# Reordering the seven products of a Strassen-form MLP: first product kept in PSUM, sums taken off GpSimd, norms placed under products

## The chip, the cores and the metric

One core of a Trainium2 chip runs the whole program. The metric is the device time of one execution in microseconds; the median of three runs of the kernel before is 2013.3 us (2011.71 to 2015.76). The profile is one more execution, of 2016.24 us.

## The reference

Two transformer blocks over 1024 tokens of width 1024, in float32. What the change touches is the MLP of the first block and the two norms behind it:

```python
    h = rmsnorm(x, ln2[l])
    gate, up = jnp.split(jnp.einsum('btd,df->btf', h, w_gu[l]), 2, axis=-1)   # 1024 -> 2 x 2816
    x = x + jnp.einsum('btf,fd->btd', jax.nn.silu(gate) * up, w_down[l])      # 2816 -> 1024
  return rmsnorm(x, ln_f)
  # second block begins:
  h = rmsnorm_2(x, norm_g[i]);  u = h @ w_in   # MLA projections
```

Before the MLP stand an input projection, a pooling mixer, a gated linear attention and a forgetting attention; behind it the second block's attention and its output. They are the same in both kernels.

## The kernel before, in words

A float32 product is made of three matmuls on pairs (hi, lo): every operand is cut by `split` (L181) into hi, a ScalarE cast to fp32r (L185), and lo, a VectorE subtraction (L186); hi·hi, hi·lo and lo·hi are added in PSUM.

Both halves of the MLP multiply 2x2 block matrices with seven products in place of eight (Winograd's form of Strassen). **Gate/up** (L1049 to L1360): the activations, transposed to features by tokens, are cut in two along features and along tokens; the four quarters and their sums are called A11, A12, A22, S1 to S4. `sums` (L1143) and `more_sums` (L1161) make them for four 128-token blocks, the second with GpSimd (L1164 to L1166). The weights come in 22 blocks: `gates` and `ups` load a block's raw weights, `w_sums` (L1234) makes four sums on VectorE, `cut_w` and `cut_t4` split them into a ring of four slots (two in pool `wg`, two in `mr`; a block takes three, w0 to w2, besides t4). `ahead(n + 1, step)` puts these steps for the next block between the products of the present one. `products(n)` (L1283) makes the seven products of block n, 12 matmuls of 128x128 by 128x512 each, into three PSUM banks a, b, c, in the order A11 (a), S2 (b), A12 (a), S3 (b), S1 (c), A22 (b), S4 (c). Bank a is read after A11 by a ScalarE copy, X; U2 = X + b after S2, U3 = X + b after S3, g2 = X + b after A22, and two sums with c, are VectorE additions; two SiLUs are ScalarE's. In the first two blocks S2 comes behind A12. GpSimd multiplies gate by up, makes the seven activation sums of the down half in a tile q, and SyncE's queue writes them to DRAM (`a_s`).

**Down** (L1362): seven products again, each of 11 k-blocks of 128, 12 matmuls a k-block, taken in pairs (groups g = 0 to 5, the last with one). `operands(j, g)` loads a pair of `a_s`, and splits it and the pair of weight rows; it is issued one group ahead. The raw quarters of `w_down` (B11, B21, B12, B22, 3 transfers each) and x1, the residual, come by SyncE's queue: B11 and B21 first, x1 during product 0, B22 and B12 before product 1. `sums23` and `sums41` make weight sums in place on VectorE. The first product, bank a, is copied by ScalarE and added by GpSimd to three places of x1 (L1413, twelve additions); the others are added by VectorE (L1405). Banks: a for products 0 and 1, b for 2, 3 and 6, c for 4 and 5.

**The norms.** For each 128-token block tb, `norm_f` squares on ScalarE (L202), takes the root by a tiny VectorE step and GpSimd (L203, L204), scales on VectorE (L1433) and stores x3 from ScalarE's queue; `norm_g` squares again, multiplies by a gain on GpSimd (L1439) and scales on ScalarE (L1440); `turn` makes eight TensorE transposes (L214) and four splits. tb 0 to 3 stand under product 6, tb 4 to 7 behind it. The first MLA products (token half 0 of two z blocks, 48 matmuls) need tb 0 to 3, the next (token half 1) need tb 4 to 7.

The order on each engine is set when the program is built, by a scheduler that walks the text: text order is priority, `urgent` gives more, and an instruction that is ready in the scheduler's own timing may be put ahead of one that waits. Once built, each engine's queue is fixed.

Of the kernel before, what the change touches and what calls it, by code (L numbers as in the profile page):

```python
# [25 lines left out]
def f(ap):  # L26
    return ap.bitcast(F32)
# [137 lines left out]
class K:  # L165
# [883 lines left out]
    def proj_o(self):  # L1049
# [85 lines left out]
        def cut(name, i, x):  # L1135
            o = slice(i * P, i * P + P)
            self.split(*[a[:, :, o] for a in self.hq[name]], x)
# [5 lines left out]
        def sums(i):  # L1143
# [8 lines left out]
            s3 = tp.tile([P, 4, P], F32, tag="U3", name="s3")  # L1152
            s2[i] = tp.tile([P, 4, P], F32, tag=("U2", "g2", "up", "up")[i], name="s2", bufs=(1, 1, 2, 2)[i])
# [5 lines left out]
            cut("S3", i, s3)  # L1159

        def more_sums(i):  # L1161

            a, b = both("A12", i)
# [3 lines left out]
            cut("S1", i, t[i][:, 0])  # L1167
            cut("A22", i, t[i][:, 1])
            cut("S4", i, s2[i])
        run0, run1 = self.products(0), self.products(1)  # L1170
# [6 lines left out]
        next(run0)  # L1177
# [3 lines left out]
        next(run0)  # L1181
        sums(2)
        next(run1)
        sums(3)
        next(run1)
        self.cut_t4(0)
        self.cut_w(0, 2)
        for i in range(4):
            more_sums(i)
        hp_cm.close()  # L1190
        self.tq = self.b2_cm.enter_context(self.pool("mq"))
        self.ups(1)
        self.w_sums(1)
        for j in range(2):
            self.cut_w(1, j, 1)
        for n, run in ((0, run0), (1, run1)):
            for step in range(5):
                next(run)
                if n == 0 and step == 2:
                    self.cut_w(1, 2)  # L1200
                    self.cut_t4(1)
                    self.gates(2)
                    self.ups(2)
                elif n == 1:
                    self.ahead(2, step)
            next(run, None)
# [76 lines left out]
    def products(self, n):  # L1283
# [3 lines left out]
        early = n < 2  # L1287

        def tmp(tag, bufs=1):
            return tp.tile([P, 512], F32, tag=tag, name=tag, bufs=bufs)  # L1290
        a, st = self.pm.tile([P, 512], F32, tag="mm", name="mma"), {}
        self.quarter(a, w[n][0], 0, "A11", last=False)
        X = tmp("X", 2)
        with self.urgent():
            nc.scalar.copy(X, a)
        if early:
            yield
        else:
            yield from self.inner(n, X, st, tmp, 0)
        self.quarter(a, w[n][1], 0, "A12", first=False)  # L1300
        sg = tmp("sg", 2)
        nc.scalar.activation(sg, a, AF.Silu)
        yield
        if early:
            yield from self.inner(n, X, st, tmp, 0)
        yield from self.inner(n, X, st, tmp, 1)
        b = st["b"]
        c = self.pm.tile([P, 512], F32, tag="mm", name="mmc")
        self.quarter(c, w[n][2], 0, "S1", last=False)
        up2, up1, g2 = tmp("up", 2), tmp("up", 2), tmp("g2")  # L1310
        with self.urgent():
            V.tensor_tensor(up2, st["U3"], c, ALU.add)
        yield
        self.quarter(b, w[n][3], 0, "A22", first=False)
        with self.urgent():
            V.tensor_tensor(g2, X, b, ALU.add)
        nc.scalar.activation(g2, g2, AF.Silu)
        yield
        self.quarter(c, w[n][2], 512, "S4", first=False)
        with self.urgent():  # L1320
            V.tensor_tensor(up1, st["U2"], c, ALU.add)
# [19 lines left out]
    def inner(self, n, X, st, tmp, step):  # L1341
        V, w = self.nc.vector, self.gw
        if step == 0:
# [3 lines left out]
            with self.urgent():  # L1347
                V.tensor_tensor(st["U2"], X, b, ALU.add)
# [803 lines left out]
```

## Time and profile before

| what | us |
|---|---|
| median of three runs | 2013.3 |
| the profiled execution, its time | 2016.24 |
| its span, first to last instruction | 2014.5 |
| PE busy in it | 1899.3 (94%) |
| DVE / ACT / POOL busy | 1172.8 / 853.9 / 350.6 |
| mean granted clock | 0.971 of 2.4 GHz |

The gate/up half runs from about 553 to 1013 us, the down half to about 1256 us, and the norms of the last four token blocks to about 1292 us. PE is TensorE, DVE VectorE, ACT ScalarE, POOL GpSimd, SPq SyncE's DMA queue.

### The profile page before, as it was taken

To read this page: it belongs to the slowest core of one execution; us is meant where nothing else is said; L and a number is where in the kernel's file an instruction comes from. 1 tells how busy PE (TensorE), PEld (TensorE's weight loads), DVE (VectorE), ACT (ScalarE), POOL (GpSimd) and SP (SyncE) were. 2 spreads that over 40 slices of the span, in tenths; PEclk is the share of its full clock that TensorE was granted. 3 is DMA by queue.
4 is the path that set the end of the run, shared out by engine and by line. 5 is a ranking of instruction groups with operands and counts; after the bars stand their busy time and mean duration, and the time that the engine had idled before them with its cause. 6 is when DMAs were issued, how large, how long until landed. Compare 5 with 4: busy or idle time off the path is not lost.

```text
span 2014.5 us, 26529 instructions
## 1 busy us (share of the span) xinstructions
PE 1899.3 (94%) x10046; PEld 1614.0 (80%) x10046; DVE 1172.8 (58%) x1838; ACT 853.9 (42%) x1670; POOL 350.6 (17%) x268
## 2 busy tenths in 40 slices
PE   6999899999959999999987999799999999999998
PEld 6887689987847888888875877697989999878886
DVE  6345545894387556555458556434278778783434
ACT  5412235782152232232222335522277777772322
POOL 1022210000043233242341003211101101000000
PEclk9999999999969999999998999799999999999999
DMA  5113345645113232322493233304043433527112
GB/s 180 41 42 126 105 139 129 154 102 188 42 52 110 95 120 89 105 105 99 140 345 114 96 95 107 115 23 147 14 106 93 93 75 88 129 79 246 63 43 104
DMA packets 90207, 218.48 MB, mean 108 GB/s; under 512 B 11184, under 2 KB 15200, under 8 KB 90064
## 3 DMA queue, kind: packets, MB, share of 16 engines
q1 hardware_dynamic: 84064, 203.20, 32.8%
q10 hardware_dynamic: 6016, 13.59, 2.0%
q8 instruction: 79, 1.29, 0.3%
q14 instruction: 48, 0.39, 0.1%
HBM read 145.36 MB, written 54.74 MB: 99 GB/s over the span
## 4 chain that ended last, share of the span: by engine, by line
PE 73%; DVE 8%; ACT 6%; issue 5%; DMA 4%; POOL 3%; SPq 0%; ACTq 0%; POOLq 0%; DVEq 0%
PE mm L193 11%; PE mm L195 11%; PE mm L194 11%; PE mmb L1280 9%; PE mmd L1504 7%; PE mmc L1280 5%; PE mma L1280 5%; PE O L731 4%; PE tps L706 3%; PE S L1768 1%; DVE wlo L186 1%; PE S L1769 1%; PE S L1770 1%; ACT P L697 1%; ACT pth L719 1%
## 5 line engine op out<-in xcount | busy, mean ns | idle before, releaser
L185 ACT CAST whi<-wst 128x1024 fp32r<-128x1024 f32 (+3 forms) x165 | 160.5, 978 | 370.7 <-PE mmd L1504 120.4
L186 DVE TENSOR_TENSOR wlo<-wst,whi 128x1024 fp32r<-128x1024 f32 (+3 forms) x165 | 213.1, 1295 | 174.5 <-ACT whi L185 171.3
L717 DVE TENSOR_TENSOR ptl<-tps,pth 128x512 fp32r<-128x512 f32 (+2 forms) x312 | 151.6, 519 | 24.3 <-ACT pth L719 22.4
L697 ACT ACTIVATE P<-S,m 128x128 f32<-128x128 f32 (+3 forms) x192 | 144.1, 752 | 30.1 <-DVE m L691 24.4
L691 DVE TENSOR_REDUCE m<-S 128x1 f32<-128x128 f32 (+3 forms) x192 | 140.2, 749 | 21.8 <-PE S L1770 17.0
L204 POOL TENSOR_TENSOR rr<-ss,mhalf 128x1 f32<-128x1 f32 x64 | 36.4, 572 | 663.6 <-DVE ss L203 658.9
L193 PE MATMUL mm<-t,whi 128*128 128x512 f32 x352 | 144.1, 410 | 3.7 <-ACT whi L185 3.7
L194 PE MATMUL mm<-t,whi 128*128 128x512 f32 x352 | 142.6, 405 | 0.0
L195 PE MATMUL mm<-t,wlo 128*128 128x512 f32 x352 | 142.1, 404 | 0.4 <-DVE wlo L186 0.4
L719 ACT CAST pth<-tps 128x512 fp32r<-128x512 f32 (+2 forms) x312 | 128.0, 461 | 30.3 <-PE tps L706 27.8
L1504 PE MATMUL mmd<-wlo,whi 128*128 128x512 f32 x308 | 123.4, 401 | 14.6 <-DVE wlo L186 13.8
L193 PE MATMUL mm<-whi,t 128*128 128x512 f32 (+1 forms) x336 | 126.4, 376 | 1.3 <-DVE og L999 1.0
L706 PE MATMUL tps<-ident,P 128*128 128x128 f32 x864 | 123.4, 277 | 4.1 <-DVE ptl L717 2.9
L1280 PE MATMUL mmb<-t,whi 128*128 128x512 f32 x352 | 112.8, 401 | 14.4 <-ACT t L185 12.0
L195 PE MATMUL mm<-whi,t 128*128 128x512 f32 (+1 forms) x336 | 125.0, 373 | 0.0
L1504 PE MATMUL mmd<-whi 128*128 128x512 f32 x308 | 118.6, 394 | 6.4 <-ACT whi L185 6.4
L194 PE MATMUL mm<-wlo,t 128*128 128x512 f32 (+1 forms) x336 | 124.3, 370 | 0.0
L1504 PE MATMUL mmd<-whi,wlo 128*128 128x512 f32 x308 | 122.3, 397 | 0.0
L1280 PE MATMUL mma<-t,whi 128*128 128x512 f32 x352 | 111.4, 398 | 7.9 <-DVE t L1241 7.7
L706 PEld LDWEIGHTS tps<-ident,P 128*128 128x128 f32 x864 | 97.5, 142 | 11.5 <-DVE ptl L717 2.9
L1280 PEld LDWEIGHTS mmb<-t,whi 128*128 128x128 f32 x352 | 67.4, 192 | 31.7 <-ACT t L185 12.4
L193 PEld LDWEIGHTS mm<-t,whi 128*128 128x128 f32 x352 | 68.8, 196 | 21.5 <-ACT whi L185 4.8
(395 smaller groups left out, 4821.8 us busy)
## 6 DMA issues: line engine op xcount, KB each, us to landing
as<-q SPq DMA_DIRECT2D x77, 256.0 KB
wst<-as SPq DMA_DIRECT2D x35, 512.0 KB
wst<-in_w_gu_dram SPq DMA_DIRECT2D x44, 256.0 KB
wst<-in_w_gu_dram SPq DMA_DIRECT2D x22, 512.0 KB
x<-in_x_dram SPq DMA_DIRECT2D x16, 512.0 KB
wst<-in_win_s_dram SPq DMA_DIRECT2D x14, 512.0 KB
Q<-qk SPq DMA_DIRECT2D x24, 256.0 KB
K<-qk SPq DMA_DIRECT2D x24, 256.0 KB
```

The source lines that it names most:

```text
L185: nc.scalar.copy(hi, src)
L186: nc.vector.tensor_tensor(lo, src, f(hi), ALU.subtract)
L193: mm(ps, lh, rh, start=first, stop=False)
L194: mm(ps, lh, rl, start=False, stop=False)
L195: mm(ps, ll, rh, start=False, stop=last)
L691: nc.vector.tensor_reduce(m, S[:, o:o + (i + 1) * P], axis=AX.X, op=ALU.max, negate=True)
L697: nc.scalar.activation(st["P", h, u][:, x:x + n], st["S", h, u][:, o:o + n], AF.Exp, bias=st.pop(("m", h, i)), accum_out=H[h][4][:, i:i + 1])
L706: nc.tensor.transpose(ps[:, x, :], st["P", h, u][:, o:o + P], self.ident)
L717: nc.vector.tensor_tensor(v[1], ps[:, x0:x1, :], f(v[0]), ALU.subtract)
L719: nc.scalar.copy(v[0], ps[:, x0:x1, :])
L1280: self.nc.tensor.matmul(ps, x[:, c], y[:, k, :], start=first and k + n == 0, stop=last and k == 3 and n == 2, skip_group_check=True)
L1504: nc.tensor.matmul(ps[t], x[:, ts], y[:, cs], start=start and k + i + m == 0, stop=k + i == 10 and m == 2, skip_group_check=True)
```

## The change

- **Gate/up, order.** A11 goes to bank b and stays there: X is a ScalarE copy of it, and S2, S3 and A22 are accumulated on top. A12 goes to bank a alone, and X += a is a VectorE addition before the SiLU. U2 and U3 become ScalarE copies of b, g2's SiLU reads b itself. A block reads PSUM five times by ScalarE (with SiLUs) and three by VectorE, where it was three by each with one more SiLU from SBUF and two more VectorE additions. The order is A11, A12, S2, S3, S1, A22, S4.
- **First two blocks.** Their products alternate; S1 and S4's activation sums are made by VectorE, and all that follows the sums of the fourth token block is put behind its last cut on ScalarE's and VectorE's queues.
- **Down.** Order and banks: 0 (b), 1 (a), 5 (c), 2 (b), 4 (d), 3 (b), 6 (b). The first product stays in b, product 4 is added to two places, GpSimd's twelve additions are gone. The transfers of weights and x1 are spread over the groups. k loops outside the token blocks; the last group of product 6 goes token block by token block.
- **Norms.** tb 0 to 3 stand under products 5 and 6, half a step apart; `norm_g` is one VectorE operation (no GpSimd, no ScalarE scaling); x3 is stored from SyncE's queue; three h buffers of their own.

```diff
@@ proj_o: first blocks @@
         def more_sums(i):
-            a, b = both("A12", i)
-            G.tensor_tensor(t[i][:, 0], t[i][:, 0], t[i][:, 1], ALU.add)
-            G.tensor_tensor(s2[i], a, s2[i], ALU.subtract)
-            G.tensor_tensor(s2[i], s2[i], b, ALU.add)
+            V.tensor_tensor(t[i][:, 0], t[i][:, 0], t[i][:, 1], ALU.add)
             cut("S1", i, t[i][:, 0])
-            cut("A22", i, t[i][:, 1])
+        def last_sums(i):
+            a, b = both("A12", i)
+            V.tensor_tensor(s2[i], a, s2[i], ALU.subtract)
+            V.tensor_tensor(s2[i], s2[i], b, ALU.add)
             cut("S4", i, s2[i])
...
+        act, dve = sums(3)
+        next(runs[1])
+        with self.tc.issue_after(act), self.tc.issue_after(dve):
+            self.ups(1)
+            self.w_sums(1)
+            for j in range(2):
+                self.cut_w(1, j, 1)
+            for n in range(2):
+                next(runs[n])
+                self.cut_w(n, 2)
+            for i in range(4):
+                more_sums(i)
+            for n in range(2):
+                next(runs[n])
+            self.cut_t4(0)
+            for i in range(4):
+                cut("A22", i, t[i][:, 1])
...
@@ products @@
+        self.quarter(b, w[n][0], 0, "A11", last=False)
+        X = read("X", b)
...
+            self.quarter(a, w[n][1], 0, "A12")
             yield
+        plus(X, a)
+        A.activation(X, X, AF.Silu)
         yield
+        self.quarter(b, w[n][0], 512, "S2", first=False, last=False)
+        U2 = read("U2", b)
+        yield
+        self.quarter(b, w[n][1], 512, "S3", first=False, last=False)
+        U3 = read("U3", b)
+        yield
+        c = bank("mmc")
         self.quarter(c, w[n][2], 0, "S1", last=False)
+        plus(U3, c)
         yield
         self.quarter(b, w[n][3], 0, "A22", first=False)
+            A.activation(g2, b, AF.Silu)
         yield
         self.quarter(c, w[n][2], 512, "S4", first=False)
+        plus(U2, c)
...
@@ down @@
-        plan = [(0, "B11", "a", True, first), (1, "B21", "a", False, adds(0, L)), (2, "B11", "b", True, adds(0, H)),
-                (3, "B12", "b", False, adds(4, H)), (4, "B11", "c", True, adds(4, H)),
-                (5, "B22", "c", False, adds(0, H)), (6, "B21", "b", False, adds(4, L))]
+        plan = [(0, "B11", "b", True, adds((0, L))), (1, "B21", "a", True, adds((0, L))),
+                (5, "B22", "c", True, adds((0, H))), (2, "B11", "b", False, adds((0, H))),
+                (4, "B11", "d", True, adds((0, H), (4, H))), (3, "B12", "b", False, adds((4, H))),
+                (6, "B21", "b", False, None)]
+        transfers = {(0, 0): ("B21", 0), (0, 1): ("B21", 4), (0, 2): ("B21", 8), (0, 3): (0, 1), (0, 4): (2, 3),
+                     (1, 0): ("B22", 0), (1, 1): ("B12", 0), (1, 2): ("B22", 4), (1, 3): ("B12", 4),
+                     (1, 4): ("B22", 8), (1, 5): ("B12", 8), (2, 1): (4, 5), (2, 2): (6, 7)}
...
-            nc.scalar.dma_start(self.x3_s[tb], x)
+            nc.sync.dma_start(self.x3_s[tb], x)
...
-            G.tensor_tensor(hs[tb], x1[tb], self.gn, ALU.mult)
-            nc.scalar.activation(hs[tb], hs[tb], AF.Copy, scale=r)
+            V.scalar_tensor_tensor(hs[tb], x1[tb], r, self.gn, ALU.mult, ALU.mult)
...
+                if j >= 5:
+                    norms(g + 6 * (j - 5))
...
+        for t in range(4):
+            with self.urgent():
+                V.tensor_tensor(x1[4 + t][:, L], x1[4 + t][:, L], ps[t], ALU.add)
```

## Rows read from the trace of the kernel before

**Rows 1.** The head of the profile page: the span, TensorE's busy time, and TensorE's granted clock in 40 equal slices of the span (tenths of full speed).

```profile
span 2014.5 us, 26529 instructions
PE 1899.3 (94%) x10046; PEld 1614.0 (80%) x10046; DVE 1172.8 (58%) x1838; ACT 853.9 (42%) x1670; POOL 350.6 (17%) x268
...
PEclk9999999999969999999998999799999999999999
```

**Rows 2.** The view of busy time by stretches, six stretches of the two MLP halves. Columns: the stretch (us from the span's start), its length, then busy us (and instructions) of PE, weight loads, DVE, ACT, POOL, then the granted clock, the share of the DMA engines, GB/s.

```profile
553.40:626.10 72.70, 49.70 (x194) 37.81 (x193) 58.76 (x72) 31.59 (x51) 28.52 (x17) 0.79 0.21 69
626.10:1010.00 383.90, 382.87 (x1668) 312.52 (x1667) 218.28 (x252) 109.53 (x137) 127.95 (x80) 1.00 0.31 110
1013.40:1043.60 30.20, 30.20 (x133) 24.59 (x131) 11.05 (x10) 9.95 (x12) 7.88 (x7) 1.00 0.85 324
1043.60:1071.70 28.10, 9.83 (x30) 6.93 (x29) 26.26 (x15) 6.47 (x7) 22.41 (x12) 0.70 0.66 242
1096.00:1245.00 149.00, 147.10 (x648) 119.47 (x646) 89.15 (x94) 61.90 (x72) 8.93 (x7) 1.00 0.30 97
1256.30:1292.20 35.90, 21.00 (x89) 16.37 (x89) 17.41 (x26) 21.43 (x34) 15.00 (x13) 0.74 0.37 124
```

**Rows 3.** The view of waits of PE over the whole span: who waited for whom, us in total, times, the longest.

```profile
PE mmd L1504 <- DVE wlo L186: 13.8, 5, 10.1
PE mmb L1280 <- ACT t L185: 12.0, 1, 12.0
PE tps L214 <- ACT h L1440: 11.0, 4, 5.6
```

**Rows 4.** Timeline rows of the first two blocks of gate/up, six moments: start us, length us, engine, line, operation; in brackets the idle time before it and what ended it.

```profile
556.92 0.68 DVE L1155 TENSOR_TENSOR s<-t,ht 128x512 f32<-128x512 f32 x1
...
562.48 1.75 DVE L1239 TENSOR_TENSOR wst<-wst 128x512 f32<-128x512 f32 x1
...
567.49 0.68 DVE L1242 TENSOR_TENSOR wst<-wst 128x512 f32<-128x512 f32 x1
...
581.52 0.69 DVE L186 TENSOR_TENSOR t<-s,t 128x512 fp32r<-128x512 f32 x1 [4.92 <-ACT t L185]
...
579.13 0.62 ACT L185 CAST vh<-s 128x512 fp32r<-128x512 f32 x1 [2.93 <-POOL s L1166]
...
590.33 0.79 PE L1280 MATMUL mmb<-t,whi 128*128 128x512 f32 x1 [11.98 <-ACT t L185]
```

**Rows 5.** Timeline of PE around the read of U2 in the second block: the last of four S1 products, and the first S3 products after it.

```profile
613.96 0.39 PE L1280 MATMUL mmc<-uh,whi 128*128 128x512 f32 x1
616.12 0.73 PE L1280 MATMUL mmb<-t,whi 128*128 128x512 f32 x2 [1.77 <-DVE U L1348]
```

**Rows 6.** The view of the tile mma: its copy by ScalarE (min/median/max ns); then the timeline row of PE that followed such a copy directly.

```profile
L1295 ACT COPY X<-mma x22: 586/587/591, 556.6 to 997.1; 128x512 f32<-128x512 f32 x22
...
575.27 0.74 PE L1280 MATMUL mma<-t,whi 128*128 128x512 f32 x2 [0.24 <-ACT X L1295]
```

**Rows 7.** The steady blocks: a timeline row of ScalarE and one of VectorE at the end of one S2 product, and two rows of the waits from 640 to 1000 us (us, times, longest).

```profile
806.91 1.05 ACT L185 CAST whi<-wst 128x1024 fp32r<-128x1024 f32 x1 [1.95 <-PE mmb L1280]
...
807.15 0.69 DVE L1348 TENSOR_TENSOR U<-X,mmb 128x512 f32<-128x512 f32 x1 [2.31 <-PE mmb L1280]
...
ACT whi L185 <- PE mmb L1280: 68.2, 35, 2.0
...
DVE wst L1239 <- DMA wst<-in_w_gu_dram: 70.3, 18, 4.9
```

**Rows 8.** Timeline rows of the start of the down half, by engine: PE, GpSimd, VectorE, ScalarE and the queue of SyncE.

```profile
1060.43 1.20 PE L1504 MATMUL mmd<-whi 128*128 128x512 f32 x4 [3.60 <-ACT whi L185]
...
1071.68 0.80 PE L1504 MATMUL mmd<-wlo,whi 128*128 128x512 f32 x1 [10.06 <-DVE wlo L186]
...
1042.32 23.69 POOL L1413 TENSOR_TENSOR x<-x,X 128x512 f32<-128x512 f32 x12 [22.16 <-ACT X L1411]
...
1049.28 4.52 DVE L1391 TENSOR_TENSOR t<-t,t 128x1024 f32<-128x1024 f32 x2
...
1073.83 1.21 DVE L1392 TENSOR_TENSOR R<-t,R 128x1024 f32<-128x1024 f32 x1
...
1058.38 1.04 ACT L185 CAST whi<-wst 128x1024 fp32r<-128x1024 f32 x1 [12.03 <-DMA wst<-as]
...
1035.26 10.20 SPq L1385 DMA_DIRECT2D t<-in_w_down_dram  x5
```

**Rows 9.** The view of PE's waits from 1090 to 1257 us.

```profile
PE mmd L1504 <- DVE wlo L186: 1.9, 3, 0.9
```

**Rows 10.** The end of the down half: one timeline row of PE and two of VectorE, then two groups of the view by line from 1256 to 1294 us (count, busy us, mean ns of one).

```profile
1274.60 1.03 PE L214 MATMUL tps<-ident,h 128*128 128x128 f32 x8
...
1285.08 1.97 PE L214 MATMUL tps<-ident,h 128*128 128x128 f32 x8 [5.65 <-ACT h L1440]
...
1271.56 3.43 DVE L1433 SCALAR_TENSOR_TENSOR x<-x,rr,gf 128x1024 f32<-128x1024 f32 x1 [2.32 <-POOL rr L204]
...
1279.85 1.28 DVE L1433 SCALAR_TENSOR_TENSOR x<-x,rr,gf 128x1024 f32<-128x1024 f32 x1 [0.73 <-POOL rr L204]
...
L1439 POOL TENSOR_TENSOR h<-x,gn 128x1024 f32<-128x1024 f32 x5 | 12.9, 2578 | 9.5 <-ACT h L202 9.5
...
L202 ACT ACTIVATE h<-x 128x1024 f32<-128x1024 f32 x8 | 8.4, 1051 | 4.0 <-DVE x L1433 3.6 <-DVE wlo L186 0.3
```

More of the change, by code (lines that the diff above doesn't have):

```diff
@@ L1176, in proj_o @@
         sums(0)
-        next(run0)
+        next(runs[0])
         self.cut_w(1, 0, 0)
@@ L1180, in proj_o @@
         sums(1)
-        next(run0)
+        next(runs[0])
         sums(2)
[L1183 to L1206, printed above, removed]
+        next(runs[1])
+        act, dve = sums(3)
+        next(runs[1])
+        with self.tc.issue_after(act), self.tc.issue_after(dve):
[13 more added lines that the diff above has]
+                cut("A22", i, t[i][:, 1])
+            self.gates(2)
+            self.ups(2)
+            for n in range(2):
+                next(runs[n])
+            for i in range(4):
+                last_sums(i)
+            hp_cm.close()
+            self.tq = self.b2_cm.enter_context(self.pool("mq"))
+            next(runs[0])
+            next(runs[0])
+            self.cut_t4(1)
+            self.ahead(2, 0)
+            next(runs[0], None)
+            next(runs[1])
+            self.ahead(2, 1)
+            self.ahead(2, 3)
+            next(runs[1])
+            self.ahead(2, 4)
+            next(runs[1], None)
     def ring(self):
@@ L1286, in products, with tmp, bank @@
         nc, V, w, tp = self.nc, self.nc.vector, self.gw, self.tp
-        early = n < 2
-        def tmp(tag, bufs=1):
+        A = nc.scalar
+        def tmp(tag, bufs=2):
             return tp.tile([P, 512], F32, tag=tag, name=tag, bufs=bufs)
[L1291 to L1296, printed above, removed]
+        def bank(name):
+            return self.pm.tile([P, 512], F32, tag="mm", name=name)
@@ L1297, in products, with read, plus @@
+        def read(tag, ps):
+            x = tmp(tag)
+            with self.urgent():
+                A.copy(x, ps)
+            return x
+        def plus(x, ps):
+            with self.urgent():
+                V.tensor_tensor(x, x, ps, ALU.add)
+        b, a = bank("mmb"), bank("mma")
+        self.quarter(b, w[n][0], 0, "A11", last=False)
+        X = read("X", b)
+        if n < 2:
             yield
+            self.quarter(a, w[n][1], 0, "A12")
         else:
-            yield from self.inner(n, X, st, tmp, 0)
@@ L1511, in down @@
+                if j >= 5:
+                    norms(g + 6 * (j - 5))
+            if then is not None:
+                then(ps)
         self.fetch()
         self.fetch()
-        for step in range(4, 10):
-            norms(step, range(4, 8))
+        for t in range(4):
+            with self.urgent():
+                V.tensor_tensor(x1[4 + t][:, L], x1[4 + t][:, L], ps[t], ALU.add)
+        for at in range(6):
+            for lag, st in enumerate((norm_f, norm_g, turn)):
+                if at - lag in range(4):
+                    st(4 + at - lag)
```

189 lines of the change are left out of this document (80 added, 109 removed).

## The prediction, made before the result was known

> **What bounds the kernel now.** I read the head of the page first, then the busy time by stretches, then PE's waits, and last the timeline of each hole. TensorE is busy 1899.3 of 2014.5 us, so only its holes can be won, and the granted clock falls to 6, 8 and 7 tenths in three slices [rows 1]. The stretches say where in the MLP the holes are [rows 2]. The twenty steady gate/up blocks have none: 382.87 us busy of 383.90. 20 x 84 matmuls in 383.9 us make 0.2285 us a matmul, which I use as the full-speed pitch. Three stretches are poor: the first two blocks (49.70 of 72.70 us busy, clock 0.79), 28 us in the second product of down (9.83 busy, clock 0.70), and the tail of down (21.00 of 35.90 busy, 0.74). A stretch at 1.2 GHz counts as busy too, so I take the loss from instruction counts. The waits agree: the longest are 10.1, 12.0 and 5.6 us, one in each hole [rows 3].
>
> **First two blocks.** They hold 168 matmuls, 38.4 us at the pitch, and 32 transposes, 4.1 us at 1.03 per eight [rows 10]; they take 72.7 us. The largest hole ends at 590.33, when S2 gets the last cut of the sums [rows 4]. Why that is late stands in the same group: VectorE takes 1.75 us for a 128x512 addition while GpSimd runs one, 0.68 without; ScalarE's cast of S4 waits for GpSimd's L1166 at the head of its queue, and VectorE then sits idle 4.92 us behind ScalarE. The change takes twelve GpSimd sums out and forbids later work ahead of these cuts.
> New length, by VectorE's count: 4 blocks x 5 operations (S2, S3), 4 x 2 (S1), 4 cuts (A22), 4 x 3 (S4), two `w_sums` of 4, six half cuts, two t4 cuts, six PSUM additions: 66 x 0.68 = 44.9 us, plus two w2 cuts at 1.21 [rows 8], 47.3 us. VectorE makes its first sum at 556.9 [rows 4]; hand-offs to ScalarE and the first weights cost some 3 us, and the last products run behind the last cut, 24 x 0.2285 = 5.5 us, of which part is VectorE work counted already; I take 2 us. End: 556.9 + 47.3 + 3 + 2 = 609 in place of 626.1. **Gain 17 us.** Bounds: 22 if PE binds (28 VectorE operations of 0.68 stand ahead of S2, so it starts at 576; 120 matmuls are 27.4 us, 1 us of hand-off: 604), 8 if the idle 4.92 us and as much again at half clock stay. What is late next is VectorE itself: the 12 sums GpSimd made are 8.2 us of its 47.
>
> **Steady blocks.** Two VectorE additions a block go; that is worth nothing, PE does not wait there (at most 1.0 us in all can be won). But S3 now follows S2 in the same bank, and must wait until U2 is copied out. Its price: ScalarE copies 128x512 in 0.587 us, and PE started 0.05 us after such a copy (its wait was 0.24) [rows 6]: some 0.66 us. Worse, the weight slot that S2 frees sets off a ScalarE cast of 1.05 us; in the rows it starts at 806.91, 0.24 us before VectorE's read of the same product could start [rows 7]. The U2 copy, on ScalarE, queues behind that cast: 1.05 - 0.24 + 0.66, with a hand-off more 1.6 us from S2's end to S3's start. Unfilled in 20 blocks that is 32 us. It need not be unfilled: in the second block of the kernel before, S2 and S3 are also neighbours on one bank, and four S1 products stand between them in PE's queue [rows 5]; there 1.77 us were still lost as VectorE was late. S1 offers 12 matmuls, 2.7 us, and after S3 the rest of S1 and the next block's A11 (another bank) fill U3's copy. I take 0.2 us a block for where the scheduler's timing and the chip's differ, nearer the filled case as rows 5 show the mechanism at work: **loss 4 us**, bounds +1 gain to 32 loss.
> The Trainium skill ("TensorE: Matmul & The Clock Gate", architectural detail) says that ScalarE and VectorE are strict FIFO, and (Part 3, the mechanism) that matmuls start and end in program order. By that rule nothing on the chip fills the gap, only the built order can; it is what makes the first rival below, and this trace agrees as far as the 1.77 us stall goes.
>
> **Start of down.** Stretch 1013.4 to 1256.3: 924 matmuls x 0.2285 = 211.1 us, 24 transposes 3.1 us, actual 242.9: 28.7 us lost. The rows name three causes [rows 8]: GpSimd's twelve additions last 23.69 us, and VectorE's 128x1024 sums beside them take 2.26 each where they take 1.21 alone; the next `a_s` pair arrives 12.03 us late for ScalarE, since 10.20 us of w_down transfers stand ahead of it in SyncE's queue; and hi/lo cuts queue behind six weight sums, the wait of 10.06. After the change GpSimd does nothing here. SyncE issues per group one 512 KB pair and 1 MB of the rest; at 324 GB/s [rows 2] that is 4.8 us beside 24 matmuls, 5.5 us: hidden, with little to spare. VectorE has per group two cuts (2.4), in six groups two sums (2.4) as well: 4.9 of 5.5 us; four PSUM additions, 2.7 us, must also fit near the change from product 1 to product 5, where bank c reuses a's PSUM. Today's boundaries, with as many sums, cost at most 0.9 us each [rows 9]. I leave 4.2 us for six of them. The transposes of tb 3 now stand inside, 1 us. 28.7 - 4.2 is **a gain of 24.5 us**, the transposes being time that the tail is relieved of; bounds 27 (boundaries as now, 1.9 us) and 18 (a full VectorE backlog of 2.7 + 4.9 us at the handover, and half clock after it, 2 us).
> Moved instructions: x3 stores leave ScalarE's queue for SyncE's; behind them there stand only later loads with slack. tb 0 to 3 under products 5 and 6 give VectorE 4 x (2 x 1.28 + 2 x 0.69 + 0.3) = 17 us more over 60, beside 27 of cuts: covered.
>
> **Tail.** From the last product to the first MLA matmul that needs tb 4 to 7: 35.9 us [rows 2]. Each norm now goes through GpSimd for 2.6 us and once more through ScalarE, and GpSimd's reads slow L1433 from 1.28 to 3.43 [rows 10]; PE waits up to 5.65 us for it. After: VectorE has 8 scalings x 1.28, 8 small ones x 0.15, 8 cuts x 0.69 [rows 4], two weight cuts x 1.21 and the last PSUM addition, 20.0 us; ScalarE has 8 squares of 1.05 and 10 casts, less. PE's own work, 48 matmuls and 32 transposes, is 15.1. So about 20 us with VectorE as the bound, and 2 us of hand-offs: **gain 14 us**; bounds 20 (PE's 15.1 plus nothing) and 8 (each of six steps 4.6 us, as PE's largest wait and its transposes, 1.03, nearly are now).
>
> **Sum.** 17 + 24.5 + 14 - 4 = 51.5 us. The profiled execution took 2016.24 us, its span and 1.7 us around it: it becomes 1964.7. The median of the runs is 2.9 us below the profiled one: **1962 us**.
>
> **Rivals.**
> (1) PSUM reads show in every block: S1 doesn't fill, 1.1 us a block (between 0.66 and 1.6), 22 us in 20 blocks in place of 4: 1962 + 18 = 1980. For it: matmuls queue in order, the cast ahead of U2 [rows 7]. Against: rows 5. Chance 0.17.
> (2) VectorE's load eats the first blocks: the first gain is 5 in place of 17: 1974. For it: 47 us of VectorE work beside 42 of PE's. Chance 0.10.
> (3) The transfers do not come in the written order: those into SBUF that gate/up still holds block SyncE's queue ahead of `a_s`, and the start of down stalls as now: 24.5 lost, 1986. For it: rows 8 show a 12 us late pair behind such a queue. Chance 0.06.
> (4) Slower: in ScalarE's queue the U2 copy gets behind a cast whose weights are still in flight. VectorE's weight sums wait up to 4.9 us for DMA, 3.9 on average [rows 7]. At 3.9 us a block, S3 would stop for 78 us in all and nothing that is ready could fill it: 1962 - 4 + 78 = 2036. It decides from 2.8 us a block (55.5 us gained over 20). Against: today's casts in these blocks wait for PE 35 times and hardly for DMA. Chance 0.05.
>
> **Numbers.** Likeliest, as summed, 0.62; its own range is 1948 to 1977 (the bounds of each hole do not fall together). With rivals 1 to 3 the range for 8 in 10 is 1946 to 1990. Less than 0.2%, 4 us, cannot be told from no change here. Faster 0.91: the likeliest, rivals 1 to 3 but for their worst ends; same 0.03; slower 0.06, rival 4 and a little more.
>
> **What would show it.** S2 of the first block starting near 576 rather than 590, GpSimd idle before its first gate-by-up product; PE busy at full clock through the second product of down, with VectorE's 128x1024 sums at 1.21; no GpSimd row over 1 us after the last `a_s` store; about 20 us from the last mmd matmul to token half 1. In the steady blocks PE's waits for U2 and U3 should sum to under 8 us, with S1 matmuls standing between S2 and S3. The prediction is wrong if those waits reach 20 us, or if a new wait on DMA or VectorE of over 5 us opens inside down.

## The result and the profile after

The changed kernel takes 1968.9 us (median of 4 runs, 1967.6 to 1969.8); the kernel before, run beside it, 2013.5. The ratio is 0.9777, 95% interval 0.976 to 0.9794: 44.6 us faster. The forecast was 1962 in a range of 1946 to 1990. The profiled execution took 1969.8 us, its span 1968.0 (before: 2016.2 and 2014.5). Of all runs in this document one, the eighth of experiment 4, took 3134 us at a mean granted clock of 0.556; experiment 4's median is of its other nine.

The head of the page after, the lines that answer to [rows 1], with PE's busy tenths in the same 40 slices:

```profile
span 1968.0 us, 26521 instructions
PE 1892.3 (96%) x10046; PEld 1602.9 (81%) x10046; DVE 1151.0 (58%) x1822; ACT 862.5 (44%) x1702; POOL 280.4 (14%) x236
...
PE   6999899999979999999999999999999999999998
...
PEclk9999999999989999999999999999999999999999
```

PE's row of the page before:

```profile
PE   6999899999959999999987999799999999999998
```

Of the three dips of the row before (5 in slice 12, 8 and 7 in slices 21 and 22, 7 in slice 26) one is left, a 7 in slice 12, and the granted clock's row has one 8 where it had 6, 8 and 7. To see what each part gave, I cut both profiles at the same first matmuls. Blocks are numbered from 0 here; S4 is a block's last product.

| from PE's first matmul of | to that of | before, us | after, us | gain | forecast |
|---|---|---|---|---|---|
| (start) | A11 of block 0 | 553.5 | 554.6 | -1.1 | 0 |
| A11 of block 0 | A11 of block 2 (the expectations have 72.6, up to the last matmul of block 1) | 72.9 | 63.6 | 9.3 | 17 |
| A11 of block 2 | first product of down | 387.1 | 391.7 | -4.7 | -4 |
| first product of down | its last matmul | 242.5 | 220.0 | 22.5 | 24.5 |
| last matmul of down | token half 1 of z | 36.3 | 19.0 | 17.3 | 14 |
| token half 1 of z | end of span | 722.3 | 719.1 | 3.3 | 0 |

**First two blocks.** PE's rows of the timeline after that have idle time before them (start, length, instruction, [idle time and what ended it]), and two rows of ScalarE from the same stretch; they answer to [rows 4]:

```profile
579.05 0.49 PE L1295 MATMUL mmb<-t,whi 128*128 128x512 f32 x1 [3.14 <-ACT t L1138]
...
589.38 0.50 PE L1295 MATMUL mmc<-uh,whi 128*128 128x512 f32 x1 [2.43 <-ACT uh L1138]
591.13 0.79 PE L1295 MATMUL mmc<-ul,whi 128*128 128x512 f32 x1 [1.25 <-DVE ul L1138]
...
597.82 0.72 PE L1295 MATMUL mmb<-t,whi 128*128 128x512 f32 x2 [1.63 <-ACT U L1313]
...
595.33 1.22 ACT L1138 CAST vh<-s 128x512 fp32r<-128x512 f32 x2 [6.00 <-DVE s L1170]
597.18 1.19 ACT L1313 COPY U<-mmb 128x512 f32<-128x512 f32 x2 [0.64 <-DVE vl L1138]
```

S2 starts at 579.05 where it started at 590.33, so the cuts come earlier, as argued. But S2 of blocks 0 and 1 ended near 584 and 587, and their U2 copies ran only at 597.18, released by VectorE's `vl`, a cut of S4; S3, which adds into the same bank, starts behind them at 597.82. A U2 copy reads PSUM and has nothing to do with S4. The link is in the tags: the copy's buffer has the tag "U2" with two slots, and the S2 sums `s2[0]` and `s2[1]` hold both until S4 is cut from them.

**Steady blocks.** Counted in the kernels, a block has four PSUM reads by ScalarE and three by VectorE, where it had two and five. PE's and ScalarE's rows between S2 and S3 in one block:

```profile
802.72 0.39 PE L1295 MATMUL mmb<-t,wlo 128*128 128x512 f32 x1
802.94 0.39 PE L1295 MATMUL mmc<-uh,whi 128*128 128x512 f32 x1
...
804.32 0.40 PE L1295 MATMUL mmc<-uh,whi 128*128 128x512 f32 x1
804.56 0.71 PE L1295 MATMUL mmb<-t,whi 128*128 128x512 f32 x2
805.11 0.40 PE L1295 MATMUL mmb<-t,wlo 128*128 128x512 f32 x1
...
802.96 1.05 ACT L185 CAST whi<-wst 128x1024 fp32r<-128x1024 f32 x1 [1.14 <-PE mmb L1295]
803.91 0.58 ACT L1313 COPY U<-mmb 128x512 f32<-128x512 f32 x1
```

The copy stands behind the 1.05 us cast and ends 1.8 us after S2's last matmul began; seven S1 matmuls (802.94 to 804.32) fill the gap. From S4's last matmul of block 2 to that of block 20 a block took 19.28 us before and takes 19.49 now: 0.21 us each. It can be seen in the rows: two matmuls at 804.56 take 0.55 us to the next start where two take 0.46 elsewhere, 0.09 lost at the start of S3; the start of A22 loses as much. Neither shows as idle time. Over 18 blocks that is 3.9 us. Block 21 takes 0.45 us less than before, and from its last matmul to down's first it takes 1.35 us where it took 0.23, which makes up the 4.7 of the table's row; this last step goes with the new down (0.23 us in experiment 2, 1.54 in experiment 3).

**Down.** PE's waits from 1005 to 1232 us (total, times, longest), and the busy time of the stretches of the first and second product (length; PE, PEld, DVE, ACT and POOL busy with counts; granted clock; DMA share; GB/s):

```profile
PE mmd L1480 <- DVE x L1420: 1.4, 2, 1.2
...
PE mmd L1480 <- ACT whi L185: 1.0, 1, 1.0
PE mmd L1480 <- DVE wlo L186: 0.8, 1, 0.8
...
1010.00:1040.00 30.00, 29.16 (x127) 23.73 (x128) 13.09 (x12) 8.66 (x10) 4.37 (x3) 1.00 0.94 334
1040.00:1070.00 30.00, 30.00 (x133) 24.68 (x132) 29.83 (x31) 11.02 (x13) 0.00 (x0) 1.00 0.86 297
```

The waits for VectorE's cuts, 13.8 us in all and 10.1 at the longest [rows 3], are down to 0.8. In the second stretch VectorE is busy 29.83 of 30.00 us and PE still has no hole: just enough.

**Tail.** PE's idle times behind the last product, and VectorE's scalings (busy, mean ns):

```profile
1236.61 1.09 PE L214 MATMUL tps<-ident,h 128*128 128x128 f32 x8 [1.30 <-DVE h L1442]
...
1247.62 1.25 PE L214 MATMUL tps<-ident,h 128*128 128x128 f32 x8 [1.47 <-DVE t L186]
...
L1442 DVE SCALAR_TENSOR_TENSOR h<-x,rr,gn 128x1024 f32<-128x1024 f32 x8 | 10.3, 1283 | 4.0 <-POOL rr L204 4.0
L1436 DVE SCALAR_TENSOR_TENSOR x<-x,rr,gf 128x1024 f32<-128x1024 f32 x8 | 10.3, 1282 | 3.1 <-POOL rr L204 3.1
```

No scaling takes 3.43 us any more [rows 10], and no wait is above 1.5 us.

### The profile page after: what moved, and what is told of

Same layout as the page of the kernel before. It is cut to its first block, busy times and chain, and to the rows that moved or that the text cites. A ratio compares the mean times of both kernels' runs of the same rounds, so it can differ in the third digit from the quotient of the medians.

```text
span 1968.0 us, 26521 instructions
## 1 busy us (share of the span) xinstructions
PE 1892.3 (96%) x10046; PEld 1602.9 (81%) x10046; DVE 1151.0 (58%) x1822; ACT 862.5 (44%) x1702; POOL 280.4 (14%) x236
## 4 chain that ended last, share of the span: by engine, by line
PE 59%; DVE 6%; ACT 2%; DMA 2%; issue 1%; POOL 0%; SPq 0%; ACTq 0%; POOLq 0%; DVEq 0%
PE mmb L1295 12%; PE mmd L1480 9%; PE mm L193 6%; PE mm L195 6%; PE mm L194 6%; PE mmc L1295 6%; PE O L731 3%; PE mma L1295 3%; PE tps L706 3%; PE S L1787 2%; DVE wlo L186 1%; PE S L1788 1%; PE S L1789 1%; DMA qr<-rh 1%; DVE ptl L717 1%
## 5 line engine op out<-in xcount | busy, mean ns | idle before, releaser
L186 DVE TENSOR_TENSOR wlo<-wst,whi 128x1024 fp32r<-128x1024 f32 (+3 forms) x165 | 201.2, 1223 | 277.9 <-ACT whi L185 275.7
L1295 PE MATMUL mmb<-t,whi 128*128 128x512 f32 x528 | 169.3, 402 | 7.6 <-ACT t L1138 3.1
L719 ACT CAST pth<-tps 128x512 fp32r<-128x512 f32 (+2 forms) x312 | 128.2, 461 | 30.0 <-PE tps L706 27.4
L1295 PEld LDWEIGHTS mmb<-t,whi 128*128 128x128 f32 x528 | 98.8, 191 | 35.4 <-ACT U L1313 8.1
L1295 PE MATMUL mmb<-t,wlo 128*128 128x512 f32 x264 | 105.2, 399 | 2.3 <-DVE wlo L186 2.3
```

The source lines that it names most:

```text
L186: nc.vector.tensor_tensor(lo, src, f(hi), ALU.subtract)
L719: nc.scalar.copy(v[0], ps[:, x0:x1, :])
L1295: self.nc.tensor.matmul(ps, x[:, c], y[:, k, :], start=first and k + n == 0, stop=last and k == 3 and n == 2, skip_group_check=True)
```

## Experiments

Times are medians beside runs of the kernel before on the same chip; stretches are from each kernel's one profile. "Changed" is the kernel after.

### 2 and 3: each half of the change alone

Experiment 2 is the changed kernel with the old `down`, experiment 3 the old kernel with the new `down`.

> Gate and up of the changed kernel, down and its norms of the kernel before. Theory A (the parts add up): only the first blocks (9.0 us won) and the steady blocks with the step into down (4.4 us lost) differ from the kernel before: 2013.5 - 9.0 + 4.4 = 2009, from 2006 to 2011. Rival B (the two halves interact: the stretch behind the MLP, 3.25 us shorter in the changed kernel though its code is the same, hangs on gate and up): 2005 or less.

> Gate and up of the kernel before, down and its norms of the changed one. Theory A (the parts add up): start of down 22.5, tail 17.3 and what follows 3.25 us won of 2013.5: 1970.5, from 1968 to 1974. If A12 and S3's own banks in the steady blocks are really dearer in the changed kernel, this kernel is within 5 us of the changed one. Rival B: the last gate/up blocks of the kernel before leave the GpSimd products and the stores of the operands later, so the start of down loses part of its gain: 1976 or more.

Measured: 2003.0 us (2000.2 to 2006.6; ratio 0.9947, 0.9928 to 0.9967) and 1980.4 (1976.8 to 1984.9; 0.9832, 0.98 to 0.9863). Both of my numbers were off, in opposite directions, and both times lie where rival B put them. By these runs gate and up are worth 10.4 us (2013.5 to 2003.0) or 11.5 (1980.4 to 1968.9), down and its tail 33.1 or 34.2. In the totals the halves do add up: 10.4 + 33.1 = 43.5 of 44.6, and experiment 2's stretch behind the MLP, 722.2 us, isn't shorter. A good part of what was wrong is my table: cut from one execution each, its stretches vary. From the first A11 to down, the old code took 459.9, 462.4 and 462.2 us in the profiles of before and experiments 3 and 4; the changed code 455.3, 452.8, 454.0 and 453.9 in after and experiments 2, 7 and 8. A mean gain of 7.5, not 4.6: 10.8 in the first two blocks (72.9 to 73.9 us old, 62.2 to 63.6 new) less 3.3 from there to down's first matmul, of which 1.1 go with the new down. The rest of the 10.4 may lie in down, which in both its forms was somewhat shorter behind the new gate and up: the old down took 239.3 us there and 242.5 behind the old, the new one 219.7 to 221.1 and 222.1. These are single profiles, and why was not tried.

### 1: do the shared slots cost the first blocks their gain?

```diff
-s2[i] = tp.tile([P, 4, P], F32, tag=("U2", "U2", "g2", "g2")[i], name="s2", bufs=2)
+s2[i] = tp.tile([P, 4, P], F32, tag=("s2", "s2", "g2", "g2")[i], name="s2", bufs=2)
```

> The changed kernel, with the S2 sums of token groups 0 and 1 in buffers of their own, so that the copies of U2 in the first two blocks need not wait for the S4 cuts to let go of the slots. Theory A (the shared slots cost the first blocks what my forecast of 17 us missed): the U2 copies run right behind S2 (near 584 and 587 us of the span, 597 in the changed kernel), S3 follows them, and the stretch from the first A11 product to that of block 2 falls from 63.6 to 56 to 59 us; the time falls from 1968.9 to 1962 to 1965. Rival B (VectorE's load is the bound of this stretch): the copies come earlier, but the products behind them wait for VectorE's cuts instead; the stretch stays within 2 us of 63.6 and the time at 1967 to 1970.

Measured: 1968.5 us (1968.1 to 1970.6), no gain. The stretch did what theory A says: copies at 583.15 and 585.22, and 57.9 us to A11 of block 2 in place of 63.6 (62.2 to 62.3 in experiments 2, 7 and 8, which have the same code there). To the end of block 2 it takes 85.8 us, where these four take 82.9 to 84.3: block 2 gave it all back. SyncE's, VectorE's, ScalarE's and PE's rows there:

```profile
610.36 9.48 SPq L1361 DMA_DIRECT2D as<-q  x7
619.93 0.38 SPq L1246 DMA_DIRECT2D wst<-in_w_gu_dram  x1
...
623.67 0.69 DVE L1254 TENSOR_TENSOR wst<-wst 128x512 f32<-128x512 f32 x1 [6.06 <-DMA wst<-in_w_gu_dram]
...
625.12 1.04 ACT L185 CAST whi<-wst 128x1024 fp32r<-128x1024 f32 x1 [6.85 <-DVE wst L1255]
626.07 0.58 ACT L1313 COPY U<-mmb 128x512 f32<-128x512 f32 x1
...
626.70 1.22 PE L1295 MATMUL mmb<-t,whi 128*128 128x512 f32 x2 [5.70 <-ACT U L1313]
```

Read upwards: PE waits for block 2's U2 copy, the copy for the cast ahead of it on ScalarE, the cast for a weight sum, the sum for a transfer, and the transfer stood in SyncE's queue behind seven operand stores, each waiting for GpSimd. It is the forecast's rival 4, a U2 copy behind a cast whose weights are in flight, in one block.

### 5 and 9: the transfer ahead of the stores

> The first experiment's kernel (S2 sums of groups 0 and 1 in buffers of their own) with one more edit: the seven operand stores of the first pair of blocks stand in SyncE's queue behind the up weights of the fourth block (number 3). There the first two blocks had become 5.7 us shorter, and block 2 gave all of it back: seven stores ahead of those weights held SyncE for 9.48 us, VectorE then waited 6.06 us for them, a ScalarE cast for VectorE, and the U2 copy of block 2 stood behind that cast (PE idle 5.70 us). Theory A (this queue is what kept the gain from the total): the wait of 5.70 us goes and the time falls to 1961 to 1965. Rival B (block 2 is held by something else as well, such as VectorE beside GpSimd or the weights' slots): the end of block 2 stays near 639 us of the span and the time at 1967 to 1970.

Measured: 1967.8 us (1965.2 to 1968.2). Inconclusive: the stores were tied to a load that stood ahead of them anyway, the rows are those of experiment 1, and PE still waited 5.6 us. Experiment 9 mends it:

```diff
+self.last_up = self.nc.sync.dma_start(r3, self.I["w_gu"][2 * self.fbs[n] + 1]).ins
...
 self.ahead(2, 3)
+self.ahead(2, 4)
 next(runs[1])
-self.ahead(2, 4)
...
+behind = self.tc.issue_after(self.last_up) if n == 1 else ExitStack()
+with behind:
...
```

> As the fifth experiment meant it (S2 sums of groups 0 and 1 in buffers of their own, and the up weights of the fourth block ahead of the first seven operand stores in SyncE's queue); there the stores were tied to the load of the third block, which stood ahead of them already, so nothing moved. Now the last step of the weights of block 2 is written ahead of the S4 product of block 1, and the stores stand behind the load that block 2's U2 copy had waited for. Theory A (the queue is what kept the gain from the total): the wait of 5.6 us in block 2 goes, the S4 product of block 2 ends near 633 us of the span in place of 638.9, and the time is 1961 to 1964. Rival B (block 2 is held by something else as well, such as VectorE's backlog or the slots of the weights): the end of block 2 stays at 637 to 639, the time at 1966 to 1969.

Measured: 1968.3 us (1965.8 to 1970.6). The load is issued at 606.69 and nothing waits for it; of block 2's wait 3.62 us are left, and from the first A11 to the end of block 2 it takes 83.1 us (changed kernel 84.3, experiments 2, 7 and 8, which have the same code there, 82.9 to 83.0). Rival B. What ends last now, VectorE, ScalarE and PE:

```profile
615.62 1.77 DVE L1256 TENSOR_TENSOR t<-wst 128x512 f32<-128x512 f32 x1
...
619.55 0.67 DVE L1318 TENSOR_TENSOR X<-X,mma 128x512 f32<-128x512 f32 x1
...
620.25 0.63 ACT L1329 ACTIVATE X<-X 128x512 f32<-128x512 f32 x1 [5.18 <-DVE X L1318]
620.79 1.03 ACT L185 CAST whi<-wst 128x1024 fp32r<-128x1024 f32 x1
621.73 0.58 ACT L1313 COPY U<-mmb 128x512 f32<-128x512 f32 x1
...
616.71 0.40 PE L1295 MATMUL mmb<-t,wlo 128*128 128x512 f32 x1
...
622.36 0.73 PE L1295 MATMUL mmb<-t,whi 128*128 128x512 f32 x2 [3.62 <-ACT U L1313]
```

The weight sums, now early, run beside GpSimd's products at 1.77 us in place of 0.69; the gate's PSUM addition stands behind them, the silu waits for it at the head of ScalarE's queue, and the copy stands behind the silu and the cast. The Trainium skill ("TensorE: Matmul & The Clock Gate", architectural detail) says that ScalarE is strict FIFO; these rows agree, as the copy's own input had been ready since S2's end, near 617 us.

### 11: the copies ahead of the casts

```diff
-for n, (x, y) in enumerate(((wh, ah), (wh, al), (wl, ah))):
+for n, (x, y) in enumerate(((wh, ah), (wl, ah), (wh, al))):
```

> The changed kernel with the three matmuls of each k step of gate and up in the order hi x hi, lo x hi, hi x lo (weights by tokens; before: hi x hi, hi x lo, lo x hi), so that the last matmul of a product lets go of the high weights at the same time as of the bank, and the built order puts the U2 and U3 copies ahead of the 1.05 us cast. Theory A (the 0.21 us a block that the steady blocks lost are the two starts of a product right behind a copy, some 0.1 us each): with the copies 1 us earlier the pitch falls from 19.50 to 19.3 us and the time by 3 to 4.5 us, to 1964 to 1966. Rival B (the loss is in something else that S2's and S3's common bank brings, such as the switches between banks, or it comes back at the casts): the pitch stays at 19.45 to 19.55 and the time at 1968 to 1970.

Measured: pitch 19.32 us, as theory A says; the time 1968.5 (1964.5 to 1971.9), which alone tells nothing. ScalarE's rows in a steady block:

```profile
801.57 0.59 ACT L1313 COPY U<-mmb 128x512 f32<-128x512 f32 x1 [1.32 <-PE mmb L1295]
802.05 1.05 ACT L185 CAST whi<-wst 128x1024 fp32r<-128x1024 f32 x1
```

The copy leads, and 0.17 of the 0.21 us a block are back, 3.1 us in 18 blocks. They come back where they were lost: between 660 and 1000 us the changed kernel has steps of 0.30 to 0.33 us between the first two matmuls of S3 and of A22, here no step between gate and up matmuls is above 0.25. The total doesn't show it: in this profile blocks 0 and 1 took 65.1 us (63.6), and PE waited 2.00 us for a U copy there and 1.42 in block 2.

### 12: all of it, and the silu behind the copies

```diff
-A.copy(x, ps)
+self.last_copy = A.copy(x, ps).ins
...
 plus(X, a)
-A.activation(X, X, AF.Silu)
+if n < 2:
+    A.activation(X, X, AF.Silu)
...
 U3 = read("U3", b)
+if n >= 2:
+    with self.tc.issue_after(self.last_copy):
+        A.activation(X, X, AF.Silu)
```

> The ninth and the eleventh experiment together (own buffers for two S2 sums, the loads ahead of the stores, and the low weights second in each k step), and one edit more: in the blocks from the third on, the silu of the gate stands behind the U3 copy in ScalarE's queue. In the ninth the load came in time, but block 2 still waited 3.62 us for its U2 copy: VectorE's weight sums beside GpSimd's products took 1.66 to 1.78 us each, the gate's PSUM addition behind them ended at 620.2 us of the span, the silu waited 5.18 us for it, and the U2 copy stood behind the silu and a cast. Theory A (the copy's place in ScalarE's queue is the last thing that holds block 2): the wait of 3.6 us goes, from the first A11 product to the end of block 2's S4 it takes 79 to 81 us (83.1 to 84.3 in the ninth and the changed kernel), the pitch is 19.3 us, and the time is 1960 to 1964. Rival B (block 2 then waits for VectorE's cuts of its own weights, late for the same reason): 82 to 84 us to the end of block 2, and only the pitch is won: 1964 to 1967.

Measured: 1958.6 us (1955.6 to 1960.6), ratio to before 0.9725 (0.9705 to 0.9744), below the changed kernel's interval: a version faster than both, and 1.4 us below what theory A gave. To the end of block 2 it takes 78.6 us (9: 83.1), the pitch is 19.31. ScalarE and PE in block 2:

```profile
619.42 0.59 ACT L1313 COPY U<-mmb 128x512 f32<-128x512 f32 x1 [3.16 <-PE mmb L1295]
619.90 1.05 ACT L185 CAST whi<-wst 128x1024 fp32r<-128x1024 f32 x1
...
616.31 0.50 PE L1295 MATMUL mmb<-t,whi 128*128 128x512 f32 x1 [0.92 <-ACT X L1313]
```

The copy waits for PE alone, and the largest idle time of PE in the block is 0.92 us. Experiment 9 without the last edits won nothing, and experiment 11 alone nothing that can be told; the 10.3 us to the changed kernel's median came only when the slot, the transfer and ScalarE's order were all mended. In the rows each wait appeared when the one ahead of it was gone. Whether ScalarE's order would do alone, with the slot or the transfer left as it was, was not tried. From the first A11 to down it takes 447.1 us against a mean of 454.0, so 6.9 of the 10.3 us lie there; the rest must lie in stretches whose code is the same and which vary between executions (the one ahead of the MLP from 550.7 to 554.7 us).

### 10: the kernel before without its GpSimd sums

```diff
-G.tensor_tensor(t[i][:, 0], t[i][:, 0], t[i][:, 1], ALU.add)
-G.tensor_tensor(s2[i], a, s2[i], ALU.subtract)
-G.tensor_tensor(s2[i], s2[i], b, ALU.add)
+V.tensor_tensor(t[i][:, 0], t[i][:, 0], t[i][:, 1], ALU.add)
+V.tensor_tensor(s2[i], a, s2[i], ALU.subtract)
+V.tensor_tensor(s2[i], s2[i], b, ALU.add)
```

> The kernel before, with the twelve sums of S1 and S4 in the first blocks on VectorE in place of GpSimd, and nothing else. In the kernel before, the stretch from the first A11 product to that of block 2 is 72.6 us, in the changed one 63.6. Theory A (GpSimd's sums and what they do to VectorE's operations beside them made the hole; the new order of the products adds little): the 128x512 operations take 0.68 us throughout, the stretch falls to 64 to 67 us and the time by 5 to 9 us, to 2005 to 2009. Rival B (the order is what counts: VectorE and ScalarE still make S1 and S4 cuts ahead of S2's and S3's last ones): the stretch stays at 70 to 74 us, as VectorE only takes over 8 us of work, and the time at 2011 to 2017.

Measured: 2009.3 us (ratio 0.9981, 0.9966 to 0.9996), the stretch 66.1 us in place of 72.9: theory A in the stretch, the time 0.3 us outside what it gave. PE's longest wait is 5.6 us where it was 12.0 [rows 3]. Block 2 took 23.2 us in place of 20.8, so of 6.8 us won 4.4 were left at its end. What else the change does here brings the stretch on to 63.6 and keeps block 2 at 20.9; which of its parts does so was not tried.

### 4 and 7: the start of down

Experiment 4 is the kernel before with `first`'s additions as `V.tensor_tensor` in place of `G.tensor_tensor`. Experiment 7 is the changed kernel with the old order of transfers:

```diff
-transfers = {(0, 0): ("B21", 0), (0, 1): ("B21", 4), (0, 2): ("B21", 8), (0, 3): (0, 1), (0, 4): (2, 3),
...
+transfers = {(0, 2): (0, 1, 2, 3), (0, 4): (4, 5, 6, 7)}
...
+for k in (0, 4, 8):
+    load("B21", k)
 for j, (op, q, bank, start, then) in enumerate(plan):
+    for m in ("B22", "B12") if j == 1 else ():
+        for k in (0, 4, 8):
+            load(m, k)
```

> The kernel before, with the twelve additions behind the first product of down on VectorE in place of GpSimd, and nothing else. Theory A (at the start of down GpSimd's additions and what they do to VectorE's sums beside them cost most of the 28 us): the 128x1024 sums take 1.21 us again in place of 2.26, and 8 to 14 us go: 1999 to 2006. Rival B (the order of the transfers costs most: the pair that comes 12 us late behind the w_down transfers is still late): 0 to 3 us go, 2010 to 2014, and PE still waits some 10 us in the second product.

> The changed kernel with the transfers at the start of down in the order of the kernel before: all of B21 ahead of the first product, the eight x1 tiles in two fours, all of B22 and B12 at the start of the second product. Everything on GpSimd and VectorE stays as changed. The kernel before with only its twelve GpSimd additions on VectorE had won 7.4 us of the 22.5 between the first and last product of down. Theory A (the order of the transfers is most of the rest): an operand pair is late again behind w_down, PE waits 6 to 12 us for ScalarE or VectorE in the second product, and the time rises from 1968.9 to 1976 to 1985. Rival B (the rest is the new place of the weight sums and the free banks): at most 3 us are lost, 1967 to 1972.

Measured: 4 takes 2005.5 us (ratio 0.9965, 0.995 to 0.9979), 7.9 less: theory A, at its weak end. The sums behind the additions are at full speed, and the stretch of down falls from 242.5 to 235.1. PE's longest wait for VectorE falls from 10.1 [rows 3] to 2.2 us, but rival B's late pair is still there, 11.54 us late for ScalarE where it was 12.03 [rows 8], and PE's waits for ScalarE's casts grow from 6.4 to 8.9 us in all:

```profile
L1391 DVE TENSOR_TENSOR t<-t,t 128x1024 f32<-128x1024 f32 x5 | 5.9, 1224 | 0.0
...
1059.99 1.04 ACT L185 CAST whi<-wst 128x1024 fp32r<-128x1024 f32 x1 [11.54 <-DMA wst<-as]
...
PE mmd L1504 <- ACT whi L185: 8.9, 2, 5.9
```

7 takes 1976.4 (0.9813, 0.9798 to 0.9829): 7.5 us lost in the time, 10.0 in the stretch (219.96 to 229.95). PE's waits, four rows of VectorE, and the windows that answer to those of after:

```profile
PE mmd L1478 <- ACT whi L185: 5.7, 2, 4.7
...
1040.20 2.35 DVE L1401 TENSOR_TENSOR t<-t,t 128x1024 f32<-128x1024 f32 x2
1042.47 2.35 DVE L1402 TENSOR_TENSOR t<-t,t 128x1024 f32<-128x1024 f32 x2
1044.74 2.35 DVE L1401 TENSOR_TENSOR t<-t,t 128x1024 f32<-128x1024 f32 x2
1047.02 2.35 DVE L1402 TENSOR_TENSOR t<-t,t 128x1024 f32<-128x1024 f32 x2
...
1036.00:1066.00 30.00, 23.69 (x87) 18.10 (x86) 28.65 (x29) 8.27 (x9) 0.00 (x0) 0.83 0.67 237
```

The size is theory A's, the path not quite: eight weight sums in one run, 9.2 us, keep VectorE from the cuts, and the clock falls to 0.83 in the stretch with PE's hole. So of some 22 us, GpSimd's additions are 7 (experiment 4, in the old kernel) and the order of the transfers 10 (experiment 7, in the new one). Measured in different kernels, the two need not add. The other 5, among them the places of the weight sums, the weights' buffers and the new banks, were not tried apart.

### 8: the second half of the norms

```diff
-V.scalar_tensor_tensor(hs[tb], x1[tb], r, self.gn, ALU.mult, ALU.mult)
+G.tensor_tensor(hs[tb], x1[tb], self.gn, ALU.mult)
+nc.scalar.activation(hs[tb], hs[tb], AF.Copy, scale=r)
```

> The changed kernel with the second half of each norm as before: a GpSimd product with the gain and a ScalarE pass with the scale, in place of one VectorE operation. Theory A (this step is what made the tail of down long): VectorE's 128x1024 scalings beside GpSimd take 2 to 3.4 us again, PE waits for ScalarE's h 3 to 6 us at a time, and the stretch from the last product of down to token half 1 of z grows from 19 to 28 to 34 us: 1977 to 1985. Rival B (what shortened the tail is that token blocks 0 to 3 are done under the products): the stretch grows by less than 4 us, 1968 to 1973.

Measured: 1981.9 us (0.9844, 0.9828 to 0.986), 13.0 lost: theory A in the time. In place it is divided: the last stretch is 27.4 us (19.0), just under theory A's bounds, and the products of down, which cover token blocks 0 to 3 now, take 226.7 (220.0). PE waits at most 3.0 us for ScalarE's h:

```profile
L1436 DVE SCALAR_TENSOR_TENSOR x<-x,rr,gf 128x1024 f32<-128x1024 f32 x7 | 13.3, 1897 | 11.2 <-POOL rr L204 11.2
...
PE tps L214 <- DVE t L186: 6.3, 3, 2.9
PE tps L214 <- ACT h L1443: 3.3, 2, 3.0
```

So of the 17.3 us won in the tail this step gives 8.4. The other 9, among them the norms of token blocks 0 to 3 under the products, were not tried apart.

### 6: S1 ahead of S2

The product S1 of blocks 2 to 21 is written ahead of S2; its addition to U3 stays where it was.

> The changed kernel with the S1 product of the blocks from the third on ahead of S2, so that it can't stand between S2 and S3. Theory A (the copies of U2 and U3 cost little because PE runs S1's matmuls under them): both waits come into the open, 0.7 to 1.6 us each in 20 blocks; the pitch of a block rises from 19.50 to 20.5 to 22 us and the time from 1968.9 to 1989 to 2020. Rival B (PE doesn't need the cover, as copies are early enough or other matmuls fill in): the pitch stays at 19.4 to 19.7 and the time at 1966 to 1973.

Measured: 1971.8 us (0.9788, 0.9774 to 0.9802), pitch 19.50: rival B. In its rows the built order has put seven matmuls of the next block's A11 between S2 and S3, and the rest of it ahead of A22. Some cover is needed, but not S1's: any product on another bank will do, and the order found one.

## Why the prediction was right, and where it was off

- **In sum** right: faster, inside the range, 7 us above the forecast. By step, in the two profiles: -8 in the first blocks, -1 from block 2 to down, -2 at the start of down, +3 in the tail, +3 behind it and -1 ahead of the MLP, where the code is the same; together 46.5 us between the spans of the two profiles against 51.5. The medians lie 1.9 us closer than the spans do. That the sum comes so near is in part luck: the miss in the first blocks is made up by a tail that was sized too small and by 3 us behind it, which no term of the sum has. Of the signs named, S2 starts at 579 us (576 said), GpSimd is idle up to the first gate-by-up product, VectorE's 128x1024 sums in down take 1.22 us, and PE's idle time for U copies, two in the first three blocks, is 2.3 us (under 8 said). One sign failed: after the last `a_s` store a GpSimd row of a 128x1 operation takes 1.46 us, where none over 1 us was said.
- **First two blocks**, 17 forecast, 9.3 measured in the two profiles, 10.8 as a mean over those of experiments 2 and 3: the failed step. "By VectorE's count" adds up operations and lets the last of them set the end; I wrote "what is late next is VectorE itself". VectorE's 0.68 us was right (experiment 10 shows GpSimd's part). Left out was what a PSUM read writes to: its slot was held by a sum that S4 needed (experiment 1 shows it, 4.4 to 5.7 us), and behind that stood a queue each on SyncE and ScalarE (9 and 12). Rival 2, VectorE's load with a gain of only 5, was nearer in size, but experiment 12 has the same VectorE work and 58.2 us, 14.7 won; what keeps it 2 us from the 17 was not looked for.
- **Steady blocks**, 4 forecast, 0.21 us in each of 18 blocks, 3.9 in all, measured: right, and experiment 11 shows the cause by giving 0.17 of the 0.21 back at the very matmuls that had lost it. The 0.2 us was a guess for a difference between two timings, so that it came out so close is luck; the mechanism, S3 behind the copy with other matmuls between, is as forecast. Rival 1 (22 us) didn't come. Experiment 6 corrects the reason: S1 isn't the only cover.
- **Start of down**, 24.5 forecast, 22.5 in the two profiles; over all profiles the old code took 239.3 to 243.6 and the new one 219.7 to 222.1, so 17 to 24 are won. Right in mechanism; experiments 4 and 7 show GpSimd's additions (7 us) and the order of the transfers (10 us in the stretch, 7.5 in the time) as causes, and leave some 5 us open. The clock stayed full there (1.00 in both stretches), and rival 3 didn't come.
- **Tail**, 14 forecast, 17.3 measured: the term was under-sized. I took VectorE's 20 us as the bound plus 2 of hand-offs; the stretch is 19.0 with the hand-offs, since the squares of the first of token blocks 4 to 7 begin at 1227.5 us, ahead of the last matmul (1229.9). Experiment 8 shows the cause of 8.4 of the 17.3 us; that the norms under the products are the rest is argued.
- **Rival 4** (2036) didn't come in the changed kernel, but its mechanism did in experiment 1, once, for 5.7 us.

## What to carry to other kernels

A count of an engine's work bounds a stage from below only. Before trusting it, follow every result that lets go of a bank or a buffer to the slot that it needs, the instruction ahead of it in its queue, and the transfer behind that. When a mended wait brings nothing, look at the very next stage: here three waits stood behind each other, and the time fell only in the version with all of them mended. Where a copy should lead a cast, let go of both by the same instruction: a swap of two matmuls did that.

## What had not been expected of the hardware

- **The same program varies more than the parts that one wants to measure.** In one group of runs the kernel before took spans from 2006.0 us, at a mean granted clock of 0.979, to 2017.8 at 0.971. In the part behind the MLP, whose code is the same, before has four stretches of 40 us at a granted clock of 0.96, after two; at 0.96, between the levels of 2.4 and 1.2 GHz, such a stretch has 3.2 us at 1.2 GHz, so some 1.6 us less work. Two of them are about the 3.3 us that the table's last row gains. This gain isn't the change's: over all profiles the part behind token half 1 of z takes 717.3 to 724.7 us, from 718.7 to 722.3 in before and experiments 4 and 10, from 717.3 to 724.4 where both halves are new. What sets off these half-clock spells stays open.
- **Beside VectorE it is not always VectorE that is slow.** In experiment 1, GpSimd's first product and VectorE's weight sums beside it:

```profile
601.06 4.59 POOL L1353 TENSOR_TENSOR q<-g,U 128x512 f32<-128x512 f32 x1 [45.67 <-ACT g L1344]
...
602.61 0.70 DVE L1255 TENSOR_TENSOR wst<-wst 128x512 f32<-128x512 f32 x1
```

GpSimd took 4.59 us in place of 1.3 and VectorE kept its 0.70, while in experiment 9 such sums for the next block, beside later GpSimd products, took up to 1.78. The Trainium skill ("SBUF — State Buffer", SBUF: two separate sides) says that a VectorE operation with two SBUF inputs and a GpSimd operation that reads SBUF contend for a shared port pair, which one holds for its whole instruction while the other waits. Both rows agree with it: in the first GpSimd waited, in the second VectorE.
